# Sums of reciprocals: two rows of eight instead of four added on TensorE, and one VectorE product in every load

## The chip, the cores and the metric

The kernel runs on one core of one Trainium2 chip. The metric is the device time of one execution in microseconds (us), median of several. A run counts as slow when it is over 1.5% above the fastest of the same kernel; all others are called fast, and ratios use fast runs alone. In the profile lines PE is TensorE and PEld its loads of weights, DVE is VectorE, ACT ScalarE and POOL GpSimd; PEclk, the granted clock, is the share of full speed that the profile gives TensorE's clock. PSUM is the memory into which this kernel's matmuls write. The span in a profile is some 2 us shorter than the time.

## The reference

```python
def setup_inputs():
    batch, seq, dim = 32, 512, 1024
    return {"x": np.abs(np.random.randn(batch, seq, dim)).astype(np.float32) + 1e-6}

def reference(x):
    return np.sum(1.0 / x, axis=-1).astype(np.float32)
```

The 16384 sums are laid out as 128 partitions times 128 "rows": one row here is a tile of 128 partitions by 1024 floats, 0.52 MB.

## The kernel before

With a and b as the halves of a row, 1/a + 1/b = (a+b)/(ab). So only 512 reciprocals per partition are needed, and they are made by ScalarE as exp(-ln(ab)). Rows come in chunks of two, described by (rows, rows added by TensorE, products on VectorE):

```python
R = 40                                             # rows in the ring of loads
A, B, C = (2, 0, 0), (2, 2, 0), (2, 2, 1)
LOADS = [[A, B, A, B], [A, B, A, C]] * 5 + [[A, B], [A, C]] * 3
LAST = 104                                         # rows 104..127 have an order of their own

ppool: 4 buffers "pr" (chunks A), 4 "ps" (chunks B, C)     # products, SBUF
spool: 3 PSUM banks (s = a+b)   bpool: 1 (copy of b)   rpool: 2 x 2 (r = 1/(ab) of a chunk A)
# ... (pool declarations condensed above)

for chunks in LOADS:                               # one load: 8 rows, later 4
    keep(nc.sync.dma_start(out=xt, in_=x_v[:, c0 : c0 + n, :]))
    for m, e, v in chunks:
        for j in range(v):                         # C: TensorE copies b to PSUM, VectorE multiplies
            b = bpool.tile([P, H], f32, tag="b")
            add(b, xt[:, q + j, H:])
            keep(nc.vector.tensor_tensor(out=pr[:, j, :], in0=xt[:, q + j, :H], in1=b, op=mult))
    for (m, e, v), pr in zip(chunks, made):
        keep(nc.gpsimd.tensor_tensor(out=pr[:, v:, :], in0=..., in1=..., op=mult))   # other products
        # e rows: TensorE adds the halves into PSUM (two matmuls with the identity)
        if waiting: sum_rows(*waiting)             # VectorE sums of the chunk before
        # ScalarE: Ln over pr; Exp into r (PSUM) for A, in place for B and C
```

`sum_rows` is VectorE work: a row of A is summed at full width (1024 elements of the ring times r, used for both halves), a row of B or C at half width (512 elements of s times exp). `keep` fixes the program order on each engine. Note that the VectorE product of a load comes, in that order, ahead of the sums of the previous load's last chunk.

Of the kernel before, what the change touches and what calls it, by code (L numbers as in the profile page):

```python
# [11 lines left out]
def kernel(  # L12
# [26 lines left out]


    A, B, C = (2, 0, 0), (2, 2, 0), (2, 2, 1)
    LOADS = [[A, B, A, B], [A, B, A, C]] * 5 + [[A, B], [A, C]] * 3



# [89 lines left out]
    c0 = 0  # L135
    for chunks in LOADS:
        n = sum(m for m, _, _ in chunks)
# [153 lines left out]
```

## Time and profile before

| what | value |
|---|---|
| time before | 169.43 us (169.39 to 169.47, three runs) |
| span in the profile | 167.6 us |
| DMA | busy in all slices but the first and the last two, some 425 GB/s |
| busy: VectorE, ScalarE, GpSimd, TensorE | 122.6, 134.8, 135.7, 130.3 us |

No single engine's total comes near the span, so the table alone names no bound. Read each busy row by stage: rows 0 to 79 pass until about 111 us (the code that the change touches), rows 80 to 127 after that (untouched).

### The profile page before, as it was taken

To read this page: it belongs to the slowest core of one execution; us is meant where nothing else is said; L and a number is where in the kernel's file an instruction comes from. 1 tells how busy PE (TensorE), PEld (TensorE's weight loads), DVE (VectorE), ACT (ScalarE), POOL (GpSimd) and SP (SyncE) were. 2 spreads that over 40 slices of the span, in tenths; PEclk is the share of its full clock that TensorE was granted. 3 is DMA by queue.
4 is the path that set the end of the run, shared out by engine and by line. 5 is a ranking of instruction groups with operands and counts; after the bars stand their busy time and mean duration, and the time that the engine had idled before them with its cause. 6 is when DMAs were issued, how large, how long until landed. Compare 5 with 4: busy or idle time off the path is not lost.

```text
span 167.6 us, 1286 instructions
## 1 busy us (share of the span) xinstructions
PE 130.3 (78%) x274; PEld 50.2 (30%) x274; DVE 122.6 (73%) x267; ACT 134.8 (80%) x137; POOL 135.7 (81%) x73
## 2 busy tenths in 40 slices
PE   0007899796987959878699869977999995998990
PEld 0003343232233313322333224322343422433430
DVE  0000777758977578884788877778989899998994
ACT  3002888979789688868879788799999998999994
POOL 1007999699895999949998898999999997999630
PEclk9999999999999999999789999999999999999999
DMA  6999999999999999999999999999999999999910
GB/s 203 422 446 430 446 422 399 461 399 446 414 409 454 407 446 422 442 424 446 430 430 422 414 418 434 424 434 434 420 426 413 436 416 416 422 413 410 409 71 18
DMA packets 4615, 67.25 MB, mean 401 GB/s; under 512 B 512, under 2 KB 640, under 8 KB 1664
## 3 DMA queue, kind: packets, MB, share of 16 engines
q1 hardware_dynamic: 4608, 67.18, 94.8%
q8 instruction: 2, 0.03, 0.1%
q14 instruction: 5, 0.04, 0.1%
HBM read 67.11 MB, written 0.07 MB: 401 GB/s over the span
## 4 chain that ended last, share of the span: by engine, by line
DMA 72%; POOL 11%; ACT 9%; DVE 2%; issue 2%; PE 1%; ACTq 1%; SPq 0%; POOLq 0%
DMA ring<-in_x_dram 72%; POOL pr L158 11%; ACT pr L230 3%; ACT pr L169 2%; ACT pr L236 2%; DVE ring L109 1%; ACT r L236 1%; PE bb L99 1%; ACT r L174 1%; ACT ring L248 1%; ACTq L286 1%; DVE pr L109 0%; DVE pr L221 0%; SPq L139 0%; ACT pr L179 0%
## 5 line engine op out<-in xcount | busy, mean ns | idle before, releaser
L99 PE MATMUL s<-ring,ident 128*128 128x512 f32 x252 | 120.3, 617 | 30.7 <-DMA ring<-in_x_dram 15.2
L158 POOL TENSOR_TENSOR pr<-ring 128x1024 f32<-128x1024 f32 (+1 forms) x52 | 112.8, 2209 | 21.8 <-DMA ring<-in_x_dram 21.8
L99 PEld LDWEIGHTS s<-ring,ident 128*128 128x128 f32 x252 | 46.3, 193 | 101.8 <-issue 61.9
L169 ACT ACTIVATE pr<-pr 128x1024 f32<-128x1024 f32 x52 | 54.7, 1053 | 27.3 <-POOL pr L158 27.3
L109 DVE CUSTOM_DVE_ANT_1 pr<-ring,r 128x1024 f32<-128x1024 f32 x30 | 36.6, 1221 | 41.5 <-ACT r L174 40.8
L109 DVE CUSTOM_DVE_ANT_1 ring<-ring,r 128x1024 f32<-128x1024 f32 x34 | 41.3, 1217 | 0.0
L109 DVE CUSTOM_DVE_ANT_0 pr<-pr,s 128x512 f32<-128x512 f32 x63 | 40.9, 683 | 0.0
L179 ACT ACTIVATE pr<-pr 128x1024 f32<-128x1024 f32 x26 | 27.5, 1057 | 0.8
L174 ACT ACTIVATE r<-pr 128x1024 f32<-128x1024 f32 x26 | 26.7, 1028 | 0.8
L212 POOL TENSOR_TENSOR pr<-ring 128x512 f32<-128x512 f32 (+1 forms) x15 | 22.3, 1504 | 3.9 <-DMA ring<-in_x_dram 3.6
L230 ACT ACTIVATE pr<-pr 128x1024 f32<-128x1024 f32 (+1 forms) x14 | 12.5, 900 | 0.5 <-DVE pr L221 0.5
L109 DVE DVE_READ_ACCUMULATOR2_ANT sums<- 128x1 f32 x127 | 10.5, 83 | 0.0
L99 PE MATMUL b<-ring,ident 128*128 128x512 f32 x16 | 9.0, 646 | 0.3 <-DMA ring<-in_x_dram 0.2
L236 ACT ACTIVATE r<-pr 128x1024 f32<-128x1024 f32 (+1 forms) x8 | 6.4, 806 | 0.1
L236 ACT ACTIVATE pr<-pr 128x1024 f32<-128x1024 f32 (+1 forms) x7 | 6.0, 863 | 0.1
L147 DVE TENSOR_TENSOR pr<-ring,b 128x512 f32<-128x512 f32 x8 | 5.5, 684 | 0.7 <-PE b L99 0.7
L99 PE MATMUL bb<-ring,ident 128*128 128x512 f32 x6 | 3.4, 644 | 2.2 <-DMA ring<-in_x_dram 1.5
L99 PEld LDWEIGHTS b<-ring,ident 128*128 128x128 f32 x16 | 3.0, 207 | 6.0 <-DMA ring<-in_x_dram 4.1
L221 DVE TENSOR_TENSOR pr<-ring,bb 128x512 f32<-128x512 f32 x3 | 2.1, 688 | 0.4 <-PE bb L99 0.2
L99 PEld LDWEIGHTS bb<-ring,ident 128*128 128x128 f32 x6 | 0.9, 188 | 4.7 <-DMA ring<-in_x_dram 3.1
L70 ACT ACT_TABLE_LOAD x1 | 1.3, 1283 | 0.7 <-PEq L275 0.7
L214 DVE TENSOR_TENSOR pr<-ring 128x512 f32<-128x512 f32 x2 | 1.4, 686 | 0.0
(9 smaller groups left out, 3.2 us busy)
## 6 DMA issues: line engine op xcount, KB each, us to landing
ring<-in_x_dram SPq DMA_DIRECT2D x10, 4096.0 KB, 37.8
ring<-in_x_dram SPq DMA_DIRECT2D x7, 2048.0 KB, 37.0
ring<-in_x_dram SPq DMA_DIRECT2D x6, 1024.0 KB, 30.7
ring<-in_x_dram SPq DMA_DIRECT2D x8, 512.0 KB, 14.4
out_dram<-sums SPq DMA_DIRECT2D x1, 64.0 KB, 1.6
```

The source lines that it names most:

```text
L99: i = nc.tensor.matmul(bank, lhsT=ident, rhs=half, start=k == 0, stop=k == len(halves) - 1,)
L109: i = nc.vector.tensor_tensor_reduce(out=row if out is None else out, in0=row, in1=fac, scale=S, scalar=0.0, op0=mult, op1=plus, accum_out ...
L147: i = nc.vector.tensor_tensor(out=pr[:, j, :], in0=xt[:, q + j, :H], in1=b, op=mult)
L158: i = nc.gpsimd.tensor_tensor(out=pr[:, v:, :], in0=xc[:, v:, :H], in1=xc[:, v:, H:], op=mult)
L169: keep(nc.scalar.activation(out=pr, in_=pr, func=Ln, scale=S))
L174: nc.scalar.activation(out=r, in_=pr[:, e:, :], func=Exp, scale=-1.0)
L179: keep(nc.scalar.activation(out=r, in_=r, func=Exp, scale=-1.0))
L212: keep(nc.gpsimd.tensor_tensor(out=pr, in0=a, in1=b, op=mult))
L221: nc.vector.tensor_tensor(out=pr[:, 0, :], in0=a[:, 0, :], in1=bs[c], op=mult)
L230: keep(nc.scalar.activation(out=pr, in_=pr, func=Ln, scale=S))
L236: keep(nc.scalar.activation(out=r, in_=pr, func=Exp, scale=-1.0))
L248: keep(nc.scalar.activation(out=rows, in_=rows, func=Ln))
```

## The change

The intent is to move work about in the first 80 rows. TensorE's additions save VectorE half of a sum's width (683 ns in place of 1217 in the profile before); giving half of them up frees TensorE, and a VectorE product in every load frees GpSimd.

```diff
-    LOADS = [[A, B, A, B], [A, B, A, C]] * 5 + [[A, B], [A, C]] * 3
+    LOADS = [[A, A, A, C]] * 10 + [[A, B], [A, C]] * 3
```

## The prediction

> **What bounds the kernel now.** The kernel streams 128 row groups ("rows" below, each 128 partitions x 1024 floats, 0.52 MB) through a ring of 40. A row's sum of 1/x is the sum of (a+b)/(ab) over its two halves: GpSimd (POOL) or VectorE (DVE) makes ab, ScalarE (ACT) makes 1/(ab) by Ln and Exp, and VectorE sums either the whole 1024-wide row times 1/(ab) (chunk type A) or, where TensorE (PE) has added the halves into PSUM, 512 elements (types B and C). I read the page's busy rows in slices first, to see which engine never rests.
>
> ```profile
> PE   0007899796987959878699869977999995998990
> DVE  0000777758977578884788877778989899998994
> ACT  3002888979789688868879788799999998999994
> POOL 1007999699895999949998898999999997999630
> PEclk9999999999999999999789999999999999999999
> DMA  6999999999999999999999999999999999999910
> ```
>
> DMA is at 9 in every slice from the second to the 38th, at about 425 GB/s. VectorE, which the change loads, is at 7 to 8 until two thirds of the span and near 9 only afterwards. The chain that ended last says the same:
>
> ```profile
> DMA 72%; POOL 11%; ACT 9%; DVE 2%; issue 2%; PE 1%; ACTq 1%; SPq 0%; POOLq 0%
> ```
>
> VectorE is 2% of that chain. Its GpSimd pieces up to row 80 are a detour that leads back, through a freed ring slot, to a load. Whether such a detour costs anything depends on how early the loads are issued. The chain in order of time and the DMA issues show it:
>
> ```profile
> 44.80 38.20 DMA ring<-in_x_dram
> ...
> 90.21 36.75 DMA ring<-in_x_dram
> ```
> ```profile
> ring<-in_x_dram SPq DMA_DIRECT2D x10, 4096.0 KB, 37.8
> ```
>
> A load of eight rows takes 37.8 us from issue to landing. GpSimd's first instruction on each load comes when it lands, and its timeline has them at 13.43, 23.14, 33.08, 43.04, 53.11, ..., 92.85, 102.91 us: one load per 9.94 us ((102.91 - 13.43) / 9). So a load stands some 28 us in the queue behind others. A slot freed a few us later shortens that queue and not the stream. Stages in numbers (columns: stretch and length, then PE, PEld, DVE, ACT, POOL busy, granted PE clock, DMA share, GB/s):
>
> ```profile
> 13.40:103.00 89.60, 75.03 (x153) 28.46 (x154) 65.05 (x141) 73.92 (x71) 79.89 (x37) 0.98 1.00 428
> 103.00:112.00 9.00, 7.44 (x18) 2.91 (x17) 6.89 (x17) 7.53 (x8) 9.00 (x5) 1.00 1.01 429
> 112.00:136.00 24.00, 22.89 (x52) 9.05 (x50) 22.43 (x48) 23.62 (x25) 24.00 (x13) 1.00 1.01 426
> ```
>
> The first stretch is the nine periods of the changed rows (0 to 71). VectorE works 65.05 of 89.60 us there (73%), GpSimd 89%. From 112 on (rows 80 and up, whose code is unchanged) every engine is nearly full: lag carried into that stage would reach the end, slack before it is free.
>
> [...] Every VectorE instruction that the change adds has its second operand in PSUM (the reciprocals r, or TensorE's copy b)[...]: GpSimd's 1024-element products average 2377 ns over the kernel and 2375 ns in the stretch 20 to 100 us, beside both kinds of sums. [...] about 425 GB/s whether VectorE is 73% or 93% busy. [...]
>
> **The change part by part.** Per eight-row load the plan goes from A B A B or A B A C (five of each) to A A A C (ten). The durations, by shape (mean ns after the busy time):
>
> ```profile
> L109 DVE CUSTOM_DVE_ANT_1 ring<-ring,r 128x1024 f32<-128x1024 f32 x34 | 41.3, 1217 | 0.0
> L109 DVE CUSTOM_DVE_ANT_0 pr<-pr,s 128x512 f32<-128x512 f32 x63 | 40.9, 683 | 0.0
> L158 POOL TENSOR_TENSOR pr<-ring 128x1024 f32<-128x1024 f32 x44 | 103.0, 2377 | 21.8 <-DMA ring<-in_x_dram 21.8
> L158 POOL TENSOR_TENSOR pr<-ring 128x512 f32<-128x512 f32 x8 | 10.3, 1288 | 0.0
> L147 DVE TENSOR_TENSOR pr<-ring,b 128x512 f32<-128x512 f32 x8 | 5.5, 684 | 0.7 <-PE b L99 0.7
> ```
>
> Records overlap a little, so I use start-to-start times of VectorE's timeline: 1.145 us for a full row (52.24, 53.39, 54.53), 0.61 for a half row, 0.60 for the product. VectorE per load: A B A B is 4 x 1.145 + 4 x 0.61 = 7.02; A B A C is 7.62; A A A C is 6 x 1.145 + 2 x 0.61 + 0.60 = 8.69. In all 20 rows x 0.535 + 5 x 0.60 = +13.7 us of VectorE work, about 136 us busy in place of 122.6. A period is 9.94 us: VectorE goes from 71 to 77% of it to 87%. It still fits, with 1.25 us over.
> GpSimd: a B chunk becomes C in every second load, 9.34 us to 8.30 (timeline, four products of either kind): -5.2 us, about 130.5 busy. As each load is awaited, this is rest, not time.
> ScalarE: 20 passes of Ln and Exp per 20 chunks as before; ten Exps write PSUM (1028 ns) in place of SBUF (1057): -0.3 us.
> TensorE: 20 rows x 4 records fewer, 5 x 2 records more: 274 to 204. At 0.43 us apart that is -30 us of work, on an engine whose part of the chain is 1%.
>
> Averages don't show whether the pipeline inside a load still closes, so I laid out one load from its landing at 0. GpSimd finishes A at 2.34, A at 4.67, A at 7.0, C at 8.3. ScalarE needs 2.09 per chunk and about 0.1 to start: done at 4.5, 6.85, 9.2, 11.25 (before, load one: 17.96 - 13.43 = 4.53). VectorE takes A from 4.53 to 6.82, A from 6.86 to 9.15, A from 9.2 to 11.5. An A (2.29) is just shorter than GpSimd's pace (2.33), so VectorE never falls behind. Then comes the next load's product at 11.5 (that load landed at 9.94), C to 13.3, and VectorE rests until 14.5. The old order also ended its third chunk, the last A, at 11.46 (24.89 - 13.43). Two waits to check. The reciprocals have two PSUM buffers, and three A in a row use them tightly: the third A's Exp would start at 8.15, the first A's sums end at 6.82, 1.3 us to spare. The ring: B and C rows are last read by GpSimd and TensorE, A rows by VectorE; with the last A third in either order, an eight-row slot is freed at 11.5 both times. Only the slots that are refilled by four-row loads (first half A A, not A B) come free 2.3 us later, against the 28 us in the queue.
>
> At row 80 the last changed load is A A A C in place of A B A C: the same GpSimd and ScalarE times, and VectorE ends at the same ScalarE hand-over. So nothing is carried into the full stage. Sum on the path: 0 us from the change's 13.7 us of VectorE work, 0 us from the 30 us taken off TensorE. I predict **169.4 us**.
>
> **Rivals.** (a) VectorE becomes the bound: 8.69 of 9.94 speaks against it, 13.7 us more work on an engine already at 73% for it. Were a full row to take 1.35 us rather than 1.145, a load would need 10 us, and a deficit that grows over ten loads would come out at the end: 171 to 175 us. (b) The reciprocal buffers stall ScalarE: if VectorE were over 1.3 us late, each Exp of a third A would wait. ScalarE has 1.6 us of rest per load, so little comes of it, 170 us; against it stands the layout above. (c) TensorE's clock drops. It would work 10 x 0.43 = 4.3 of 9.94 us per load[...]. At half clock the copy b takes 1.7 us instead of 0.86, so the product waits until about 1.9 us after its load landed, 0.4 late; C's sums then end at 3.8, still before the next A at 4.5. I expect the clock to drop and the time not to. (d) Less GpSimd work makes it faster: only if GpSimd set the pace in the changed rows, but it waits for DMA in every load (21.8 us in ten waits, 12.1 of them at the start). At most 0.2 us.
>
> **Range and chances.** The three timed runs before span 0.08 us, and I know of no term on the path. I allow 0.5 us down for chip and alignment and 0.8 up, as (b), (c) or a late load near row 80 would lose before they gain: 168.9 to 170.2. A move over 2% needs 3.4 us; only (a) makes that. Chances: faster 0.01, same 0.96, slower 0.03.
>
> **What would show it.** Right: DMA still at 9 through slice 38, one load per about 9.95 us, VectorE near 136 us and GpSimd near 130.5, TensorE with 204 records, granted clock well under 0.98 in rows 0 to 79 and full after, row 80's GpSimd product near 111 us as before. Wrong: GpSimd waiting for VectorE, a wait of ScalarE's Exp on VectorE, full-row sums or GpSimd products clearly longer than 1217 and 2377 ns, or DMA slices under 9.

Two forecasts stand as my estimates: that GpSimd's product would keep its 2377 ns, and that TensorE's clock would drop with fewer additions. The trace before shows a mean granted clock of 0.988, with one stretch at 0.50, from 81.6 to 85.0 us; that is the half clock of rival (c), whose 1.7 us for the copy is 0.86 us doubled.

## The result and the profile after

The changed kernel takes 169.41 us (169.19 to 169.76, six runs), against 169.41 us (169.25 to 169.90, six runs) for the kernel before. The ratio is 0.9999, with a 95% interval from 0.9983 to 1.0016. Ratios here are the mean time of one kernel's fast runs over that of the other's of the same rounds, so they are not quite the ratio of the medians that are quoted.

The busy slices of the changed kernel:

```profile
PE 108.6 (65%) x204; PEld 43.0 (26%) x204; DVE 135.6 (81%) x272; ACT 133.9 (80%) x137; POOL 130.2 (78%) x73
...
DVE  0001797979979798998979897898699999998994
...
POOL 1007969698895969979696985999999997999630
PEclk9999999969789699957999696985899999999999
DMA  6999999999999999999999999999999999999910
```

The DMA row is the same, digit for digit. VectorE went from 7 and 8 to mostly 9 and 7 in slices 5 to 26, GpSimd fell a little there, TensorE a lot, and the granted clock has gaps that it did not have. The totals on the page: VectorE 135.6 us (before 122.6), GpSimd 130.2 (135.7), ScalarE 133.9 (134.8), TensorE 108.6 in 204 records (130.3 in 274). The same three stretches as before (stretch and length, then PE, PEld, DVE, ACT, POOL busy, granted clock, DMA share, GB/s):

```profile
13.40:103.00 89.60, 55.29 (x91) 21.21 (x92) 78.43 (x148) 74.60 (x72) 75.16 (x37) 0.88 1.00 431
103.00:112.00 9.00, 6.71 (x14) 2.69 (x12) 7.40 (x16) 7.02 (x7) 9.00 (x5) 0.88 1.02 432
112.00:136.00 24.00, 21.70 (x46) 9.24 (x46) 21.89 (x50) 23.00 (x24) 23.88 (x13) 0.86 1.00 426
```

In rows 0 to 71, VectorE works 78.43 of 89.60 us in place of 65.05, and DMA runs at 431 GB/s in place of 428. From 112 us on the picture is that of before, but for TensorE's clock. The durations, from the groups by shape:

```profile
L158 POOL TENSOR_TENSOR pr<-ring 128x1024 f32<-128x1024 f32 x39 | 91.3, 2374 | 26.6 <-DMA ring<-in_x_dram 24.2 <-DVE sums L109 2.3
...
L109 DVE CUSTOM_DVE_ANT_1 ring<-ring,r 128x1024 f32<-128x1024 f32 x44 | 53.4, 1216 | 0.0
...
L109 DVE CUSTOM_DVE_ANT_0 pr<-pr,s 128x512 f32<-128x512 f32 x43 | 27.9, 682 | 0.0
```

GpSimd's product kept its 2374 ns (2377 before) beside 20 more full-width sums, and the sums kept their 1216 and 682 ns. So none of these operations was slowed by its neighbours. One more thing is read from VectorE's timeline, in the brackets for idle time and what ended it:

```profile
104.11 0.69 DVE L147 TENSOR_TENSOR pr<-ring,b 128x512 f32<-128x512 f32 x1 [0.99 <-PE b L99]
104.71 0.68 DVE L109 CUSTOM_DVE_ANT_0 pr<-pr,s 128x512 f32<-128x512 f32 x1
105.32 0.08 DVE L109 DVE_READ_ACCUMULATOR2_ANT sums<- 128x1 f32 x1
105.32 0.68 DVE L109 CUSTOM_DVE_ANT_0 pr<-pr,s 128x512 f32<-128x512 f32 x1
105.93 0.08 DVE L109 DVE_READ_ACCUMULATOR2_ANT sums<- 128x1 f32 x1
106.62 1.22 DVE L109 CUSTOM_DVE_ANT_1 pr<-ring,r 128x1024 f32<-128x1024 f32 x1 [0.61 <-ACT r L174]
```

Here the product of a load (first line) waited 0.99 us for the copy b, the two half-width sums of the previous C followed, and the next A (last line) still had to wait 0.61 us for ScalarE. The lateness of the copy was swallowed before the next chunk.

Two times from each trace carry the rest of this document: when VectorE begins the first sum of row 80, and when it ends its last sum.

| run | row 80 begins | last sum ends | between |
|---|---|---|---|
| before | 116.19 | 165.11 | 48.91 |
| after | 115.34 | 164.66 | 49.32 |

The 0.85 us between the two at row 80 is no gain from the change. By GpSimd's first product on each load, loads are 9.7 to 9.8 us apart in four of nine gaps before and in seven of nine after; the longest gap is 10.61 us before and 10.56 after. How many longer ones there are differs between profiled runs (in before four more, of 9.94 to 10.07; after one more, of 10.04), and the timed runs show no difference.

### The profile page after: what moved, and what is told of

Its sections match the earlier page's. It is cut to its first block, busy times and chain, and to the rows that moved or that the text cites. A ratio compares the mean times of both kernels' runs of the same rounds, so it can differ in the third digit from the quotient of the medians.

```text
span 167.1 us, 1139 instructions
## 1 busy us (share of the span) xinstructions
PE 108.6 (65%) x204; PEld 43.0 (26%) x204; DVE 135.6 (81%) x272; ACT 133.9 (80%) x137; POOL 130.2 (78%) x73
## 4 chain that ended last, share of the span: by engine, by line
DMA 67%; POOL 12%; ACT 7%; issue 6%; DVE 4%; SPq 1%; PE 1%; ACTq 1%; POOLq 0%
DMA ring<-in_x_dram 67%; POOL pr L158 12%; ACT pr L230 3%; DVE ring L109 2%; ACT pr L236 2%; DVE pr L109 2%; SPq L139 1%; ACT r L236 1%; PE bb L99 1%; ACT pr L169 1%; ACT ring L248 1%; ACT r L174 1%; ACTq L286 1%; DVE pr L221 0%; DVE sums L109 0%
## 5 line engine op out<-in xcount | busy, mean ns | idle before, releaser
L158 POOL TENSOR_TENSOR pr<-ring 128x1024 f32<-128x1024 f32 (+1 forms) x52 | 107.2, 2102 | 26.6 <-DMA ring<-in_x_dram 24.2
L99 PE MATMUL s<-ring,ident 128*128 128x512 f32 x172 | 89.5, 669 | 5.8 <-DVE sums L109 5.5
L169 ACT ACTIVATE pr<-pr 128x1024 f32<-128x1024 f32 x52 | 54.7, 1051 | 27.8 <-POOL pr L158 27.1
L109 DVE CUSTOM_DVE_ANT_1 pr<-ring,r 128x1024 f32<-128x1024 f32 x40 | 48.8, 1221 | 10.2 <-ACT r L174 9.8
L109 DVE CUSTOM_DVE_ANT_1 ring<-ring,r 128x1024 f32<-128x1024 f32 x44 | 53.4, 1216 | 0.0
L99 PEld LDWEIGHTS s<-ring,ident 128*128 128x128 f32 x172 | 36.8, 218 | 58.7 <-issue 41.2
L99 PE MATMUL b<-ring,ident 128*128 128x512 f32 x26 | 19.0, 820 | 46.8 <-DMA ring<-in_x_dram 46.8
L174 ACT ACTIVATE r<-pr 128x1024 f32<-128x1024 f32 x36 | 37.0, 1028 | 1.1
L109 DVE CUSTOM_DVE_ANT_0 pr<-pr,s 128x512 f32<-128x512 f32 x43 | 27.9, 682 | 0.0
L147 DVE TENSOR_TENSOR pr<-ring,b 128x512 f32<-128x512 f32 x13 | 8.9, 685 | 18.5 <-PE b L99 18.5
L179 ACT ACTIVATE pr<-pr 128x1024 f32<-128x1024 f32 x16 | 16.9, 1058 | 0.5
## 6 DMA issues: line engine op xcount, KB each, us to landing
ring<-in_x_dram SPq DMA_DIRECT2D x10, 4096.0 KB, 37.1
```

What stands on the lines that cost most here:

```text
L99: i = nc.tensor.matmul(bank, lhsT=ident, rhs=half, start=k == 0, stop=k == len(halves) - 1,)
L109: i = nc.vector.tensor_tensor_reduce(out=row if out is None else out, in0=row, in1=fac, scale=S, scalar=0.0, op0=mult, op1=plus, accum_out ...
L147: i = nc.vector.tensor_tensor(out=pr[:, j, :], in0=xt[:, q + j, :H], in1=b, op=mult)
L158: i = nc.gpsimd.tensor_tensor(out=pr[:, v:, :], in0=xc[:, v:, :H], in1=xc[:, v:, H:], op=mult)
L169: keep(nc.scalar.activation(out=pr, in_=pr, func=Ln, scale=S))
L174: nc.scalar.activation(out=r, in_=pr[:, e:, :], func=Exp, scale=-1.0)
```

## The experiments

Twelve kernels ran, in three groups, each with the kernel before on the same chip. "Row 80" is VectorE's first sum of row 80, and "period" the start-to-start time of a load's first sum.

**1. The product part alone.**

```diff
-    LOADS = [[A, A, A, C]] * 10 + ...
+    LOADS = [[A, B, A, C]] * 10 + ...
```

> The product part alone: every load A B A C, so VectorE gets 5 products more (+3.0 us) and GpSimd 5 half products less (-5.2 us), and TensorE keeps four rows of eight. Theory (the DMA stream sets the changed rows, all engine work there is under its period of 9.9 us): 169.4 us, ratio 0.998 to 1.002. Rival (the equal time is a gain from lighter GpSimd cancelled by a loss on VectorE): this part alone is the gain, so about 167 to 168.5 us.

Measured: 169.23 us (before 169.42), ratio 0.999 (0.9973 to 1.0006). VectorE 125.8 us busy, GpSimd 130.3.

**2. The additions alone.**

```diff
-    LOADS = [[A, A, A, C]] * 10 + ...
+    LOADS = [[A, A, A, B], [A, A, A, C]] * 5 + ...
```

> The other part alone: loads A A A B and A A A C in turn, so TensorE adds two rows of eight, but only every second load has a VectorE product. VectorE gets +10.7 us, GpSimd nothing less. Theory: 169.4 us, ratio 0.998 to 1.002. Rival (two parts that cancel): this part alone is the loss, 170.5 to 172 us. TensorE's granted clock should fall to about 0.9, as with the whole change.

Measured: 169.59 us, ratio 1.000 (0.9983 to 1.0016); VectorE 132.7 us, granted clock 0.878. Neither part moves the time. So the equal time is not a gain and a loss that cancel: each part is hidden by itself.

**3. VectorE filled to just under the load's period.** A fourth kind of chunk, both rows summed at full width and one product on VectorE.

```diff
-    A, B, C = (2, 0, 0), (2, 2, 0), (2, 2, 1)
-    LOADS = [[A, A, A, C]] * 10 + ...
+    A, B, C, D_ = (2, 0, 0), (2, 2, 0), (2, 2, 1), (2, 0, 1)
+    LOADS = [[A, A, A, D_]] * 10 + ...
```

> TensorE adds no row at all in the first 80: A A A and a chunk whose two rows are both summed at full width, one of its products on VectorE. VectorE has 8 x 1.145 + 0.60 = 9.76 us per load, just under the DMA period of 9.8 to 9.9. Theory: VectorE has almost no rest in slices 5 to 26, yet the time is 169.4 us, at most 170. Rival (the slack on VectorE is smaller than I laid out, or its lag at row 80 counts): 171 us or more.

Measured: 169.29 us, ratio 0.9992 (0.9964 to 1.002). The period is 9.73 us in seven of nine loads, against 9.71 to 9.73 in most of the changed kernel's; row 80 begins at 115.49. VectorE's slices:

```profile
DVE  0001699999999999999999999999976999999994
```

This is the edge and not just under it: from the second load to row 80 VectorE has no rest but two waits for a copy, 0.5 us together, and its 9.73 us per load are level with the transfer. An engine at 9 for half of the kernel, with some 22 us more work than before (144.4 against 122.6), cost nothing here: a load's work, at 9.73 us, was no longer than the load's transfer.

**4. VectorE over the period: two products.**

```diff
+    LOADS = [[A, D_, A, D_]] * 10 + ...
```

> Two products per load on VectorE and all rows summed at full width: 8 x 1.145 + 2 x 0.605 = 10.37 us per load, over the DMA period. Theory: VectorE falls behind by about 0.5 us per load and enters row 80 some 4 to 5 us late; the last stage can make up about 2 us of it in VectorE's gaps, so 171.5 to 174 us, slower. Rival (the DMA stream sets everything, VectorE's lag is swallowed by the ring): 169.4 us.

Measured: 195.71 us, ratio 1.1538 (1.1516 to 1.1561). Slower as the theory said, but by 26 us in place of 2 to 5, so the expectation failed in size. The trace shows why. First VectorE, then TensorE, in one load:

```profile
51.02 0.68 DVE L147 TENSOR_TENSOR pr<-ring,b 128x512 f32<-128x512 f32 x1
53.87 0.69 DVE L147 TENSOR_TENSOR pr<-ring,b 128x512 f32<-128x512 f32 x1 [2.17 <-PE b L99]
54.47 1.21 DVE L109 CUSTOM_DVE_ANT_1 pr<-ring,r 128x1024 f32<-128x1024 f32 x1
```
```profile
51.75 2.08 PE L99 MATMUL b<-ring,ident 128*128 128x512 f32 x2 [7.15 <-DVE pr L147]
54.61 2.07 PE L99 MATMUL b<-ring,ident 128*128 128x512 f32 x2 [0.78 <-DVE pr L147]
```

The first product ends, and the second waits 2.17 us for its copy b. There is one PSUM buffer for b: TensorE began the second copy at 51.75 us, once the first had been read (that product ended at 51.70), and then took 2.08 us for its two records. The same copy took 2.08 us in the changed kernel at a granted clock of 0.50 (at 91.43 us), and 1.13 at 1.00 (at 52.58). The period was 12.59 us: 10.42 of VectorE work and 2.17 of waiting. Row 80 began at 141.41 in place of 115.34, 26.07 us late, and the time rose by 26.3 us: the last stage made up nothing of it. I had counted on about 2 us. The clock row on this page shows 9 in slice 11, where the first of these ran; that does not fit its 2.08 us, see the last section.

**5. Two products again, without the wait for the buffer.** In these rows the three PSUM banks of the additions are idle, so the copies take those. The edit is shown against experiment 4.

```diff
-                b = bpool.tile([P, H], f32, tag="b")
+                if e:
+                    b = bpool.tile([P, H], f32, tag="b")
+                else:
+                    b = spool.tile([P, H], f32, tag="s")
```

> The kernel with two products on VectorE per load and full-width sums once more, but its copies b take the three PSUM buffers of the row additions, idle in these rows, in place of the single one. Theory (of the 26 us that it lost, 2.17 us per load were VectorE waiting for the second copy, which could not start before the first was read and then ran at half clock; only about 0.5 us per load was its own work): VectorE 10.4 us per load with no wait before the second product, row 80's first sum near 120.5 us, time 173.5 to 175.5 us. Rival (full-width sums or products beside GpSimd take longer than I count): 180 us or more.

Measured: 175.84 us (before in this group 170.36, with runs from 169.42 to 172.80, the last of them slow), ratio 1.0324 (1.0279 to 1.037). The period is 10.42 us in all loads but the first (11.84). The second product waited 1.02 us for its copy in each of the first two loads, and not at all from the third on. Row 80 began at 122.24, 6.9 us later than in the changed kernel. The time is 0.3 us over the range that I gave (by the ratio it rose by 5.5 us), and the first period accounts for 1.4 us of the lag. So of the 26 us of experiment 4, about 19 (26.1 less 6.9) came from the single buffer that is refilled in 2.08 us, and the rest from VectorE's own work past the period. How much of the 19 is the buffer and how much the slow copy, these runs don't part.

**6. VectorE's cost in the changed kernel itself, raised.** Two full-width sums of each load run twice.

```diff
+            twice = c < 80 and c % 8 in (0, 2) and j == e
+            for _ in range(1 + twice):
                 sum_row(...)
```

> The changed kernel, but in two of a load's three A chunks the first row's full-width sum runs twice (same operands, same result): VectorE 8.69 + 2 x 1.145 = 10.98 us per load, nothing else touched. Theory (VectorE has 9.72 - 8.69 = 1.0 us of rest per load, and its lag at row 80 comes out whole at the end, as VectorE took 49.0 to 49.3 us from row 80's first sum to the end in every run so far): first sum of row 80 near 127 us in place of 115.3, time 180 to 181.5 us. Rival (the ring or the last stage swallows lag): 175 us or less.

Measured: 183.19 us, ratio 1.0759 (1.0703 to 1.0815). The time is above the range that I gave, 180 to 181.5. The period was 11.19 us, not 10.98, and row 80 began at 129.18. The missing 0.2 us per load comes from the edit: a repeated sum starts some 0.1 us later than back to back (at 52.70 and 56.24, where the sums before them would have let it at 52.58 and 56.13). It writes the same tile as its first run; that it waits for that write is my estimate and was not shown. The other full-width sums follow each other within 1.15 us. It isn't the buffer rival of the prediction, though ScalarE's Exp does wait for VectorE here, which it doesn't in the changed kernel (total us, times, longest):

```profile
ACT r L176 <- DVE sums L109: 25.3, 10, 3.1
```

After the wait at 55.16 the Exp is done at 56.19, and VectorE comes to that chunk only at 58.53; its only wait for ScalarE up to row 80 is that for the first load. So the two buffers held ScalarE up here (25.3 us in ten waits) and cost no time, with VectorE late. The lag at row 80 is 13.84 us; by the ratio the time rose by 12.9 us (0.0759 x 169.4). It comes out at the end nearly whole.

**7 and 8. The DMA stream made lighter, in both kernels.** Wrong results on purpose: two rows of eight are stale in the loads of rows 40 to 79.

```diff
-        keep(nc.sync.dma_start(out=xt, in_=x_v[:, c0 : c0 + n, :]))
+        d = 6 if 40 <= c0 < 80 else n
+        keep(nc.sync.dma_start(out=xt[:, :d, :], in_=x_v[:, c0 : c0 + d, :]))
```

> The kernel before, but the loads of rows 40 to 79 bring six rows of eight (wrong result on purpose: two rows of each are stale), so the DMA period there is 7.45 us in place of 9.94 and the engines have the same work. Theory: the DMA stream was the bound, and GpSimd (9.34 and 8.30 us by turns, mean 8.8) takes its place; row 80 is reached about 5 us earlier, and some 2 us of the waits for DMA in the last stage go too: 162 to 165 us. Rival (an engine or a hand-over sets the pace already): under 1 us gained.

> The changed kernel with the same lighter loads (wrong result on purpose). VectorE at 8.69 us per load is then the bound, where before it was GpSimd at 8.8. Theory: 162 to 165 us, within 1% of the kernel before with lighter loads: the change trades one engine's load for another's of the same size, and the DMA hides even that. If VectorE's added 13.7 us had been hidden by DMA alone, this run would be 3 us or more longer than its partner.

Measured: 164.40 us (ratio 0.9696) for the kernel before and 161.53 us (0.9531; its runs spread from 160.54 to 162.79) for the changed one. The stream was the bound in these rows: lighten it and both kernels gain 5 us and more. With it out of the way the change would be worth 2.9 us (161.53 over 164.40 is 0.983); I had expected under 1%. With four runs each, the intervals of the two ratios (0.9678 to 0.9715 and 0.9472 to 0.9589) don't overlap. GpSimd's timeline, of the kernel before and then of the changed one:

```profile
52.71 77.31 POOL L159 TENSOR_TENSOR pr<-ring 128x1024 f32<-128x1024 f32 x36 [1.74 <-DMA ring<-in_x_dram]
```
```profile
52.66 74.04 POOL L159 TENSOR_TENSOR pr<-ring 128x1024 f32<-128x1024 f32 x36 [1.78 <-DMA ring<-in_x_dram]
```

Both run the 36 products up to row 103 without a break, in 77.31 and in 74.04 us. In the kernel before GpSimd is the next bound (periods 8.23 and 9.3 in turn), in the changed one VectorE (8.66 per load, without idle time from 58 to 112 us). Row 80 began at 110.34 and 108.69. So the 5 us taken off GpSimd are real work saved, and the DMA hides them, as it hides the 13 us put on VectorE.

**9. TensorE kept busy.** Each addition of the first 80 rows is made twice into the same bank.

```diff
+                if c0 < 80:
+                    add(s, xc[:, j, :H], xc[:, j, H:])
                 add(s, xc[:, j, :H], xc[:, j, H:])
```

> The changed kernel, but TensorE makes each addition of the first 80 rows twice into the same bank (the second overwrites the first), so it works about 7.7 us per load[...]. Theory: the granted clock comes back to 0.97 or more, the product's waits for the copy b shrink, and the time stays 169.4 us (ratio 0.998 to 1.002), as the slower clock cost nothing. Rival (the slow clock cost something that lighter engines gave back): 0.5 us or more faster.

Measured: 169.57 us, ratio 1.0009 (0.9983 to 1.0036), granted clock 0.977 over the run (changed kernel 0.906). VectorE's waits for b in rows 8 to 79 sum to 1.3 us in the changed kernel and to 0.7 us here. They shrank by half and not to nothing, and the time did not move: the slow clock in these rows (0.88 over rows 0 to 71 of the changed kernel, 0.98 here) had cost nothing. The first copy after row 79 came late here too (1.17 us of waiting, against 1.58), so the run doesn't test that one.

**10. A ring of 24 rows.** `R = 24` in place of 40.

> The changed kernel with a ring of 24 rows in place of 40. A slot is freed 11.5 us after its load's landing, and the third load after it is the one that takes it; two loads of 9.9 us are then still on their way, so about 8 us of queue are left in place of 28. Theory: 169.4 us, at most 170.5; loads issue to land in 18 us in the middle. Rival (the ring is only just long enough): 173 us or more.

Measured: 169.28 us, ratio 0.9989 (0.9966 to 1.0012). The eight-row loads took 17.5 us from issue to landing in the median, against 37.1 with 40 rows. The queue is 20 us shorter and the stream as it was.

**11. A ring of 16 rows.** `R = 16`.

> The changed kernel with a ring of 16 rows, two loads. A slot comes free 11.5 us after its load landed, and by then the one load behind it has landed as well, 9.7 us after. Theory: the DMA engines stand still some 2 us in every 9.7 and the changed rows take 1.5 to 2.5 us longer per load, so 185 to 205 us, which shows what the slots would cost if they came free too late. Rival (the slots have nothing to do with it): 169.4 us.

Measured: 215.11 us, ratio 1.2615 (1.255 to 1.268), and the result is wrong, which I had not meant: all of the last 24 rows are loaded, in program order, before the first of them is read, and 16 slots don't hold them. So only the first 80 rows of this run count, and the time, over the 185 to 205 us that I gave, does not: row 80 began at 137.59, 22.2 us late, and the stretch after it took 73.8 us in place of 49.3. In the first 80 rows the DMA row shows the gaps:

```profile
DMA  7999299995969699795989898899999999500000
```

The period was 11.5 to 13.0 us from the third load on. Slots that come free too late cost 1.8 to 3.2 us per load; with 24 rows nothing is lost.

**12. Rows 64 to 79 in loads of four.** An attempt to gain.

```diff
-    LOADS = [[A, A, A, C]] * 10 + ...
+    LOADS = [[A, A, A, C]] * 8 + [[A, A], [A, C]] * 2 + ...
```

> The changed kernel with rows 64 to 79 loaded four at a time instead of eight, same work. The engines can begin rows 76 to 79 at the same landing but with half the backlog, so VectorE should reach row 80's first sum near 111.5 us in place of 115.3. If the end were set by VectorE's 49 us after that alone, 165.6 us; but the last rows land near 159 to 160 us as before, and their Ln, Exp and sums follow, so I expect 168.3 to 169.4 us: DMA sets the end from one side and the last stage from the other.

Measured: 170.05 us (before 170.36), ratio 1.0012 (0.996 to 1.0065): no gain, and above the 168.3 to 169.4 that I gave, in a group whose kernel before is about 1 us above that of the other groups. Row 80 began at 112.60, 2.7 us earlier than in the changed kernel, and the last sum ended at 165.47 all the same. GpSimd's timeline shows where the lead went:

```profile
107.31 8.36 POOL L158 TENSOR_TENSOR pr<-ring 128x1024 f32<-128x1024 f32 x4 [0.65 <-DMA ring<-in_x_dram]
117.06 4.70 POOL L158 TENSOR_TENSOR pr<-ring 128x1024 f32<-128x1024 f32 x2 [1.39 <-DMA ring<-in_x_dram]
121.95 3.61 POOL L158 TENSOR_TENSOR pr<-ring 128x1024 f32<-128x1024 f32 x2 [0.18 <-DMA ring<-in_x_dram]
126.85 4.69 POOL L158 TENSOR_TENSOR pr<-ring 128x1024 f32<-128x1024 f32 x2 [1.29 <-DMA ring<-in_x_dram]
```

It now waits for DMA before nearly every load, 1.39 and 1.29 us at a time, where the changed kernel ran 16 products without a break.

## Why the prediction was right

**The bound.** The DMA stream sets the pace of the changed rows, as predicted. Experiments 7 and 8 show it by lightening the stream, and 1, 2 and 3 by loading the engines without effect. The row of 9s from which the prediction starts would not have shown it alone. This is the DMA row of experiment 4, where VectorE sets the pace:

```profile
DMA  6999999999999999999999999999999990000000
```

It is at 9 too, as long as there is anything left to load, for the ring let the stream run ahead of VectorE. The difference is where it ends: seven slices before the end there, two in the changed kernel. In both kernels the last sum ends 3.3 us after the last load has landed (161.82 us before, 161.40 after). The period of the prediction was a little off: I took the mean of GpSimd's first products, 9.94 us, where the usual one is 9.71 and longer gaps, five of nine in that trace, make up the mean. VectorE's rest in a usual load is therefore about 1.0 us, not 1.25. At 9.76 us by count (experiment 3), 9.73 as measured, it still fitted.

**The sum.** VectorE was forecast at about 136 us and measured 135.6; GpSimd 130.5 and 130.2; TensorE 204 records, as counted. The work arrived as it was counted and cost nothing on the path. One sign of being wrong that the prediction names, GpSimd waiting for VectorE, seems to be there: the list of waits puts one of 2.3 us before row 72's product (102.08 us) and one of 1.3 us at 138.97 down to VectorE's sums. They are waits for DMA: these loads landed at 101.95 and 138.81, and TensorE's copy from the first of them began at 101.99. A sum of VectorE happened to end in the same moment.

**The layout of one load.** Slots are freed as forecast. The sixth load is issued at 25.12 us, before at 25.13; the first four-row load at 71.65 in place of 69.88, against a forecast of 2.3 us later. Neither shows in the DMA row, and experiment 10 shows that 20 us less of queue does not show either.

**The stage after row 80.** The prediction said that lag carried into it would reach the end. In experiments 4, 5 and 6, 26.1, 6.9 and 13.8 us of lag each left 49.2 to 49.4 us from row 80 to the last sum, the 49.3 of the changed kernel. What it did not see is the other side: with an earlier row 80 (experiment 12 at 112.60, experiment 2 at 114.42) the stretch grows to 52.9 and 50.9 us, as the last rows land no sooner (at 161.60 and 161.46, against 161.40). The two limits meet within about a microsecond at the kernel's usual row 80, so lag is paid nearly one for one and a lead is worth nothing. With the stream shortened (7 and 8) the 49 us return.

**The rivals.** (a) VectorE as the bound was refuted for the changed kernel and shown for a slightly heavier one. (b) The two buffers of r did not bind; with VectorE late they made ScalarE wait, and still cost no time (6). (c) The clock fell as forecast, to 0.88 over rows 0 to 71, and in rows 8 to 79 VectorE waited up to 0.99 us for the copy, more than the 0.4 expected: two records of it take 2.08 us at a granted clock of 0.50 and 1.13 at 1.00 (at 91.43 and 52.58 us), where the prediction had 1.7 and 0.86. Experiment 9 speaks for its being free. One detail was wrong: I expected the full clock after row 79, and the granted clock was 0.50 from 111.8 to 118.6 us, after which VectorE waited 1.58 us for a copy in rows 84 to 87. That wait lies in the last stage, and no run took it away by itself. The stretch from row 80 to the end is 49.32 us with it; without it it is 48.91 in the kernel before and 49.47 in experiment 1. So it has no price that shows, but these are single traces. (d) The gain from lighter GpSimd work is nothing here. It would be 2.9 us in a kernel with the lighter stream.

## What to carry to other kernels

Where a transfer stream sets the pace of a stage, compare each engine's work per load with the time per load, not its busy share of the kernel: 8.69 us, and 9.73 as measured in experiment 3, cost nothing against 9.72; 10.42 cost the difference in every load and gave none of it back. Before moving work onto an engine, look for single buffers that it will share with a second instruction of the same kind: the wait for one PSUM buffer and its copy cost 2.2 us per load in experiment 4, three times the 0.7 us of work that was over. A change that is worth nothing under one bound can be worth something once that bound is moved, so note what it saved (here 5 us of GpSimd work) as well as that the time stood still.

## What the traces showed of the clock, and of GpSimd beside VectorE

- The clock row can miss a slow clock. In experiment 4 the mean granted clock is 1.00 in the stretch from 50 to 90 us, while a copy of two records takes 2.08 us, against 1.13 us for the same copy at a granted clock of 1.00 and 2.08 at 0.50 (the changed kernel's at 52.58 and 91.43 us). The changed kernel's own first copy, at 13.48 us, took 2.05 us where the row says 1.00. Why, no run shows. Check the clock by a matmul's duration. The stretches at 0.50 that the changed kernel's trace has before 120 us are 3.4 us long (33.3 to 36.7 is the first) or 6.8 (70.8 to 77.6 and 111.8 to 118.6).
- GpSimd's product of 1024 elements took 2377 ns before, and 2374 ns with 20 more full-width sums beside it, each with one operand in SBUF and one in PSUM.
